# Output projection of a DiT block: operand sums formed during the attention, splits issued ahead of the sums that end a product, row steps staggered by one tile

## The chip, the cores and the metric

The kernel runs on one core of one Trainium2 chip. The metric is device time in microseconds (us) of one execution; lower is better. The core has four compute engines that the profile names PE (TensorE: matmuls; its weight loads are listed as PEld), DVE (VectorE), ACT (ScalarE) and POOL (GpSimd). SP (SyncE) issues DMAs. Each engine works through its own list of instructions strictly in order: an instruction that waits holds up all that stand behind it on the same engine. Engines meet only through semaphores, and through the buffers that one fills and another empties.

## The reference

One layer of a diffusion-transformer trunk, batch 1, 1024 latent tokens of width 1024 on a 16 x 64 grid, and 256 context tokens, all in fp32:

```python
h_x = _modulate(x, g_pre_mix[l], sh1, sc1)          # RMSNorm, then scale and shift
u_x, q_x, k_x, v_x = _project(h_x, w_in[l])         # 512 pool features; 8 heads of 64
attn_x = _neighbourhood_attention(q_x, k_x, v_x, k_c, v_c, rpb[l])
mix_x = jnp.concatenate([_pool_mixer(u_x, pool_w[l], pool_scale[l]), attn_x], axis=-1) @ w_out[l]
x = x + gt1 * _rmsnorm(mix_x, g_post_mix[l])
y_x = _sq_relu_mlp(_modulate(x, g_pre_mlp[l], sh2, sc2), w_mlp_in[l], w_mlp_out[l])
x = x + gt2 * _rmsnorm(y_x, g_post_mlp[l])
```

The change concerns the line with `w_out` (the output projection), the row step behind it (`x + gt1 * _rmsnorm(...)`), and the beginning of the MLP, whose input is that row after another RMSNorm.

## The kernel before, in words

**Arithmetic.** Every fp32 product is made of three matmuls. `split` (L143, L144) makes the high part of an operand as a cast on ScalarE and the remainder as a subtraction on VectorE; `three` (L168 to L170) multiplies high by high, high by low and low by high. A weight tile goes through `high_low`, an operand tile of the projection through `out_operand`, a token tile of the MLP through `token_part`; all three call `split`.

**The output projection.** Its input is a 2 x 2 block matrix over tokens (a: the first 512, b: the last 512) and features (512 pool features in `pools`, 512 attention features in `heads`; both lists hold four pages of 128 features by 1024 tokens). It is multiplied by the 2 x 2 blocks of `w_out` with seven block products instead of eight (Strassen-Winograd). Operand A11 is the pools' half a, A12 the heads' half a, A22 the heads' half b, and four are sums: S1 of the two halves b, S2 of S1 and A11, S4 of S2 and A12, S3 of the pools' two halves. The weights of the seven are likewise single blocks or sums. These sums are made by accumulating DMAs that GpSimd's queue issues (`add_to`): the transfer adds what it brings to what stands in the destination. A product is four output tiles of 128 tokens by 512 columns, twelve matmuls each (four feature pages, three matmuls). TensorE takes the products in this order: A11 and A12 (both into `x`), S1 (`poz`), S2 (`poy`), S4 (added to `poz`), S3 (`pov`), A22 (added to `pov`). Between them VectorE combines finished products into the quarters of the result: `u2` from `y`, `s5` from `u2` and `z`, and by `out_less` the remaining ones.

**The row step.** For a quarter of an output row tile (half h of the columns, tile t) `out_kept` takes the squares' sum on ScalarE (`mean_square`, L130) and multiplies by the gate on VectorE into the page `mp1[t]`. Once both halves are there, `row_added(t)` has the root made (`rsqrt_of`: one small operation on VectorE, then a power on GpSimd, L139), adds the gated row to the input row `xr` on VectorE (L1004), stores it by a DMA of GpSimd's queue and takes the new row's squares on ScalarE. `row_scaled(t)` makes the second root in the same way and scales the row. Then TensorE transposes the row tiles in groups of eight 128 x 128 blocks (`normal_pair`, `px`, L1080): a group of two banks is read by ScalarE with scale and shift (`nf`, L1085), and split into the token operands `th` and `tl`. `last_product` interleaves the four tiles of the product A22 with the first of these groups.

**The MLP's beginning.** The MLP uses seven products too. For the first eight blocks of 128 hidden columns, the products of the first token half come first: `first_sum` (`phx`, operand B11, token pairs 0 and 1) and `second_sum` (B21 added, token pairs 2 and 3), two blocks at a time. `first_sum` copies its bank out as `s1`. The second token half is transposed (32 transposes) and combined in `second_half`, called between these sums. The product T2 (`phy`) of block 0 opens the main part. The weights of the MLP come from SP's loads and `weight_parts`, with four split tiles made ahead (`lookahead`).

**The attention.** 32 units, four pairs of heads by eight bands of columns, one unit each 3.1 us or so; `weighed(i - 4)` writes the result of a unit to `heads[j]`, and after the last band the page of pair j ("head j") is whole. GpSimd makes the bias tables of a pair of heads ahead of it (`tables`, L660).

**What sets the order.** Inside an `in_order(...)` block the instructions of the engines named keep the order in which the code issues them. `tc.issue_after` places a block behind a given instruction. Instructions outside such blocks on an engine (the MLP's weight casts on ScalarE and VectorE, for instance) are put between them by the scheduler when the program is built, and their place is then fixed too. Around the change the blocks are: `projected` (attention and A11, A12), `added` (S1 to S3 and the first row tiles), `first_part` (A22) and `whole` (last token pair). `first` keeps TensorE's order, `first_pool` GpSimd's through the attention and the operand sums. Buffers come from rotating pools (`whl` for split weights, `page` for 1024-column pages), so a split can also wait for TensorE's last use of the buffer's earlier content.

Before the change the loop of the attention makes four copies of the pools' half b (`combined_a`, SP) and adds each pair of heads to its copy as the pair is whole, which gives S1. All further sums stand behind the attention: S2 on top of S1 in `combined_a`, S4 in the heads' half a, S3 in the pools' half a.

## Time and profile before

| | before |
|---|---|
| median of 3 runs (lowest to highest) | 1078.92 us (1078.45 to 1079.13) |
| the profiled execution | 1078.19 us, span 1076.4 us |
| mean granted TensorE clock in its span | 0.987 |
| PE busy | 1040.1 us, 97% |
| DVE / ACT / POOL busy | 713.2 us, 66% / 533.9 us, 50% / 83.9 us, 8% |
| DMA | 194.87 MB, mean 181 GB/s |

How the rows are read that follow. A row of a timeline is: start in us from the beginning of the span, duration, engine, source line, operation, output <- input by the program's names (buffer numbers left out), the shape, how many instructions were drawn together, and in brackets the engine's idle time just before, with what ended it. Matmuls overlap, so a matmul's own duration is longer than the distance to the next one; in undisturbed stretches the starts are what counts. A row of the view by windows is: the window, its length, then the busy time and the number of instructions of PE, PEld, DVE, ACT and POOL, then the granted clock of TensorE, the busy share of the DMA engines and GB/s. A row of the waits is: engine, waiting instruction, releaser, total us, times, longest. In the chain of waits a row is: start, length, step. TensorE's names in the projection: `poz` (S1, S4), `poy` (S2), `pov` (S3, A22), `px` (transposes), `phx` (first and second sums of the MLP), `phy` (T2 of the MLP). For the weights `to_0` to `to_3` and `bo_0`, h is the high part, l the low and w what was loaded.

### The profile page before, as it was taken

The numbers are of one execution on the slowest core, as the hardware profiler recorded it, in microseconds if no ns is written. First come the engines' busy times: TensorE is split into PE (matmuls) and PEld (weight loads), VectorE is DVE, ScalarE is ACT, GpSimd is POOL, SyncE is SP. The second block draws the span as 40 slices with busy tenths as digits, with TensorE's granted clock in tenths as the row PEclk, the third lists the DMA queues.
The fourth block names the chain that finished last, engine by engine and source line by source line (L and its number), as shares of the span: only waits on it lengthen the run. The fifth ranks groups of instructions, "written<-read, shape, count | busy, mean of one in ns | idle before, by whom it ended". The sixth has DMA issues, their size and how long they took to land.

```text
span 1076.4 us, 15501 instructions
## 1 busy us (share of the span) xinstructions
PE 1040.1 (97%) x5878; PEld 854.3 (79%) x5878; DVE 713.2 (66%) x1115; ACT 533.9 (50%) x927; POOL 83.9 (8%) x141
## 2 busy tenths in 40 slices
PE   8999999999999985989999999999999999999997
PEld 7788888877887764768888888888888888888885
DVE  5536646627986376689988766765577657556576
ACT  7462022257887355677555555454454334334441
POOL 2020000023201422030000000000000000000001
PEclk9999999999999988999999999999999999999999
DMA  9906753021126992673776534435597775546556
GB/s 343 316 19 212 274 178 115 29 76 42 50 70 168 203 232 83 174 237 100 267 241 205 195 122 156 163 118 188 202 381 244 256 253 183 208 158 214 176 182 209
DMA packets 104315, 194.87 MB, mean 181 GB/s; under 512 B 7984, under 2 KB 42544, under 8 KB 104240
## 3 DMA queue, kind: packets, MB, share of 16 engines
q1 hardware_dynamic: 81888, 150.82, 42.6%
q10 hardware_dynamic: 16848, 30.44, 7.7%
q0 software_dynamic: 5504, 12.61, 5.3%
q8 instruction: 46, 0.75, 0.3%
q14 instruction: 29, 0.24, 0.1%
HBM read 147.70 MB, written 38.81 MB: 173 GB/s over the span
## 4 chain that ended last, share of the span: by engine, by line
PE 88%; issue 4%; DMA 3%; ACT 2%; DVE 2%; POOL 1%; SPq 0%; POOLq 0%; DVEq 0%; ACTq 0%
PE pk L404 4%; PE S L718 3%; PE pa L794 3%; PE phx L168 3%; PE phx L170 3%; PE phx L169 3%; PE pyv L169 3%; PE pyz L170 3%; PE pyz L169 3%; PE pyx L170 3%; PE phv L168 3%; PE phz L168 3%; PE pyv L170 3%; PE pyx L168 3%; PE phz L169 3%
## 5 line engine op out<-in xcount | busy, mean ns | idle before, releaser
L1194 ACT ACTIVATE c<-c 128x512 f32<-128x512 f32 x48 | 30.3, 631 | 56.0 <-DVE c L1304 22.3
L168 PE MATMUL phx<-thB,wpA 128*128 128x512 f32 x128 | 51.1, 399 | 6.9 <-ACT s L1252 5.6
L741 ACT ACTIVATE sp<-sp,nm 128x640 f32<-128x640 f32 (+1 forms) x64 | 51.4, 803 | 8.9 <-DVE nm L732 8.6
L732 DVE CUSTOM_DVE_ANT_0 sp<-S,tab 128x640 f32<-128x640 f32 (+1 forms) x56 | 42.9, 803 | 17.3 <-PE S L718 10.4
L139 POOL TENSOR_TENSOR ry<-vy,nhalf 128x1 f32<-128x1 f32 x8 | 4.4, 550 | 594.0 <-DVE vy L137 594.0
L169 PE MATMUL phx<-tlB,wpA 128*128 128x512 f32 x128 | 50.3, 393 | 0.0
L170 PE MATMUL phx<-thB,wpA 128*128 128x512 f32 x128 | 50.3, 393 | 0.0
L144 DVE TENSOR_TENSOR wpS<-S,wpS 128x512 fp32r<-128x512 f32 x64 | 43.6, 686 | 9.3 <-ACT wpS L143 9.3
L143 ACT CAST wpS<-S 128x512 fp32r<-128x512 f32 x64 | 39.2, 616 | 19.9 <-PE phv L170 8.6
L1195 ACT ACTIVATE c<-c 128x512 f32<-128x512 f32 x48 | 30.3, 632 | 11.3 <-DVE sa L1267 10.5
L168 PEld LDWEIGHTS phx<-thB,wpA 128*128 128x128 f32 x128 | 24.4, 191 | 13.0 <-ACT s L1252 6.2
L170 PEld LDWEIGHTS phx<-thB,wpA 128*128 128x128 f32 x128 | 24.3, 190 | 5.2
L169 PEld LDWEIGHTS phx<-tlB,wpA 128*128 128x128 f32 x128 | 24.5, 191 | 4.9
L718 PE MATMUL S<-kT,q 64*128 64x384 f32 (+1 forms) x128 | 27.9, 495 | 0.4 <-DVE nm L732 0.4
L1312 DVE TENSOR_TENSOR c<-phz,u 128x512 f32<-128x512 f32 x16 | 11.0, 690 | 25.6 <-PE phz L170 25.5
L794 PE MATMUL pa<-pt,v 128*64 128x128 f32 x352 | 25.9, 279 | 0.6
L779 DVE COPY pt<-T 128x512 f32<-128x512 f32 x32 | 21.9, 686 | 5.6 <-PE T L760 5.6
L168 PE MATMUL phy<-thT,wpS 128*128 128x512 f32 x64 | 24.9, 389 | 0.0
L169 PE MATMUL phy<-tlT,wpS 128*128 128x512 f32 x64 | 24.9, 389 | 0.0
L170 PE MATMUL phy<-thT,wpS 128*128 128x512 f32 x64 | 24.9, 389 | 0.0
L168 PE MATMUL phz<-thT,wpS 128*128 128x512 f32 x64 | 24.9, 389 | 0.0
L169 PE MATMUL phz<-tlT,wpS 128*128 128x512 f32 x64 | 24.9, 389 | 0.0
(1006 smaller groups left out, 3348.0 us busy)
## 6 DMA issues: line engine op xcount, KB each, us to landing
b<-in_w SPq DMA_DIRECT2D x64, 512.0 KB, 4.5
hrS<-hdS SPq DMA_DIRECT2D x32, 512.0 KB, 5.2
hrA<-hdA SPq DMA_DIRECT2D x24, 512.0 KB, 5.8
wm<-in_w_mod SPq DMA_DIRECT2D x16, 512.0 KB, 9.6
wa_0w<-in_w SPq DMA_DIRECT2D x16, 512.0 KB, 5.0
wa_1w<-in_w SPq DMA_DIRECT2D x16, 512.0 KB, 4.1
hdA<-c ACTq DMA_DIRECT2D x32, 256.0 KB, 2.1
hdS<-sa ACTq DMA_DIRECT2D x32, 256.0 KB, 3.2
```

What stands on the lines that cost most here:

```text
L143: nc.scalar.copy(hi, src)
L144: nc.vector.tensor_tensor(lo, src, hi.bitcast(F32), sub)
L168: nc.tensor.matmul(ps, ahi, bhi, start=first, stop=False, skip_group_check=more)
L169: nc.tensor.matmul(ps, ahi, blo, start=False, stop=False, skip_group_check=more)
L170: nc.tensor.matmul(ps, alo, bhi, start=False, stop=last, skip_group_check=more)
L404: nc.tensor.matmul(pks[b][j], wk(wgt, k, low, j * P, P), r, start=(k == 0 and n == 0), stop=(k == KT - 1 and n == 2))
L718: nc.tensor.matmul(S[e][:, c0 : c0 + keys.shape[1]], q[hs, cols], keys[hs], start=True, stop=True)
L732: nc.vector.tensor_tensor_reduce(out=to, in0=s, in1=bt, scale=1.0, scalar=BIG, op0=add, op1=ALU.min, accum_out=nm)
L741: nc.scalar.activation(sp, sp, AF.Exp, bias=least[i, e], scale=-1.0, accum_out=sums[i][:, e : e + 1])
L794: nc.tensor.matmul(pa[e * HD : (e + 1) * HD, cols], v[:, f : f + HD], turns[i][:, e, c] if c < 4 else fifths[i][:, :, (e + 1) * HD : (e + ...
L1194: nc.scalar.activation(r, src, AF.Relu)
L1195: nc.scalar.activation(r, r, AF.Square)
```

## The change

Five things are done.

1. The sums are formed elsewhere and at other times. S1 is formed in place in the pools' half b (`s1a`), S3 in place in the pools' half a (`s3`, added at units 1 and 2 of the attention). `sa2` begins as a copy of S3 (SP, units 5 and 6) and takes the pair of heads, which gives S2; S4 is S2 added to the heads' half a. For pairs 0 to 2 these adds are issued in the attention's loop, at `i % 8 == 3` (S1, S2) and `i % 8 == 7` (S4); for pair 3 behind it.
2. The splits of S2 and of the last S1 operand stand among the `out_kept` steps of `x` at the end of `projected`; those of S4, S3 and A22 stand ahead of the sums that end S2, S4 and S3, so that ScalarE and VectorE come to them earlier.
3. `out_kept` is taken apart into `out_square` and `out_gated`, `row_added` and `row_scaled` give up their roots to `row_root` and `row_second`. The steps of row t - 1 are issued among those of row t. All row scalings are on VectorE (two were on ScalarE).
4. `last_rows` is gone. The steps of rows 4 to 7 move into the `added` block (half 1), into `last_product` (half 0, among the tiles of A22 and the token pairs), and into `last_pair`. The row loads 4 to 7 are issued at the end of `added`.
5. `second_half(("T2",))`, which holds the 32 transposes of the second token half, is issued ahead of the second sums of blocks 2 and 3 instead of behind them.

```diff
@@ -868,7 +868,9 @@
...
         both = [page(f"ss{i}") for i in range(2)]
-        combined_a = [both[k // 2][:, (k % 2) * 512 : (k % 2) * 512 + 512] for k in range(4)]
+        sa2 = [both[k // 2][:, (k % 2) * 512 : (k % 2) * 512 + 512] for k in range(4)]
+        s3, s1a = [p[:, :512] for p in pools], [p[:, 512:] for p in pools]
@@ -883,9 +885,6 @@
...
         first_pool.__enter__()
-        for k in range(4):
-            nc.sync.dma_start(combined_a[k], pools[k][:, 512:])
         with in_order(ET.PE, ET.Activation, ET.DVE, ET.SP) as projected:
@@ -905,7 +904,18 @@
...
                     if i % 8 == 3:
-                        add_to(combined_a[i // 8 - 1], heads[i // 8 - 1][:, 512:])
+                        j = i // 8 - 1
+                        add_to(s1a[j], heads[j][:, 512:])
+                        add_to(sa2[j], heads[j][:, 512:])
+                if i in (1, 2):
+                    for k in (2 * i - 2, 2 * i - 1):
+                        add_to(s3[k], s1a[k])
+                if i in (5, 6):
+                    for k in (2 * i - 10, 2 * i - 9):
+                        nc.sync.dma_start(sa2[k], s3[k])
+                if 8 < i < N and i % 8 == 7:
+                    j = i // 8 - 1
+                    add_to(heads[j][:, :512], sa2[j])
                 low()
@@ -942,28 +952,31 @@
...
                 if i > N:
-                    out_operand("S1", i - N - 1, combined_a[i - N - 1])
+                    out_operand("S1", i - N - 1, s1a[i - N - 1])
             low()
...
                 out_sums(x[t], "A12", [wo[2], wo[3]], t, False)
-            out_operand("S1", 3, combined_a[3])
             t2 = [out_load(f"to2_{kk}w", kk, 1, wraw) for kk in (2, 3)]
...
                 add_to(t2[i], t1[i])
+            add_to(heads[3][:, :512], sa2[3])
+            for i in range(2):
                 add_to(halved(t3[i]), out_block(i, 1))
-            for k in range(4):
-                add_to(combined_a[k], pools[k][:, :512])
             for i in range(2):
                 add_to(t4[i], t2[i])
-            for k in range(4):
-                add_to(heads[k][:, :512], combined_a[k])
-            for k in range(4):
-                add_to(pools[k][:, :512], pools[k][:, 512:])
             first_pool.__exit__(None, None, None)
             wt1 = [high_low(f"to1_{t}", t1[t]) for t in range(2)]
-            for t in range(4):
-                out_kept(0, t, x[t], att.tile([P, NKEY], F32, tag="sp", name=f"jo0_{t}", bufs=6)[:, :512])
+            junk = lambda t: att.tile([P, NKEY], F32, tag="sp", name=f"jo0_{t}", bufs=6)[:, :512]
+            out_operand("S2", 0, sa2[0])
+            out_kept(0, 0, x[0], junk(0))
+            out_operand("S2", 1, sa2[1])
+            out_operand("S1", 3, s1a[3])
+            out_kept(0, 1, x[1], junk(1))
+            out_operand("S2", 2, sa2[2])
+            out_operand("S2", 3, sa2[3])
+            for t in (2, 3):
+                out_kept(0, t, x[t], junk(t))
@@ -985,8 +998,14 @@
...
-        def out_done(h, t, c):
-            out_kept(h, t, c, out_junk(h, t))
+        def out_square(h, t, c):
+            mean_square(out_junk(h, t), c, ssm[h][:, t : t + 1])
+        def out_gated(h, t, c):
+            if t not in mp1:
+                mp1[t] = page(f"mp1_{t}")
+            hs = slice(h * 512, (h + 1) * 512)
+            nc.vector.tensor_tensor(mp1[t][:, hs], c, G1[:, hs], mul)
@@ -995,70 +1014,85 @@
...
         x1d = [dram.tile([P, D], F32, tag=f"x1_{t}", name=f"x1_{t}") for t in range(NT)]
-        rows = {}
-        def row_added(t):
-            xt = rows[t]
-            rs = rsqrt_of(f"m_{t}", ssm[0][:, t : t + 1], ssm[1][:, t : t + 1])
-            nc.vector.scalar_tensor_tensor(xt, mp1[t], rs, xt, mul, add)
-            nc.gpsimd.dma_start(x1d[t], xt)
-            ms = sm(f"sx_{t}", 1, 2)
-            mean_square(mp1[t], xt, ms)
-            return ms
+        rows, root = {}, {}
...
-        def row_scaled(t, ms):
-            rn = rsqrt_of(f"n_{t}", ms)
-            if t < 2:
-                nc.scalar.activation(mp1[t], rows[t], AF.Identity, scale=rn)
-            else:
-                nc.vector.tensor_scalar_mul(mp1[t], rows[t], rn)
+        def row_root(t):
+            root[t] = rsqrt_of(f"m_{t}", ssm[0][:, t : t + 1], ssm[1][:, t : t + 1])
+        def row_added(t):
+            xt = rows[t]
+            nc.vector.scalar_tensor_tensor(xt, mp1[t], root[t], xt, mul, add)
+            nc.gpsimd.dma_start(x1d[t], xt)
+            root[t] = sm(f"sx_{t}", 1, 4)
+            mean_square(mp1[t], xt, root[t])
+        def row_second(t):
+            root[t] = rsqrt_of(f"n_{t}", root[t])
+        def row_scaled(t):
+            nc.vector.tensor_scalar_mul(mp1[t], rows[t], root[t])
...
             z = out_bank_sums("poz", "S1", wt1)
-            for k in range(4):
-                out_operand("S2", k, combined_a[k])
-            nc.scalar.copy(s5[0], z[0])
             wt2 = out_weights("to2", t2)
-            for t in (1, 2):
-                nc.scalar.copy(s5[t], z[t])
             y = out_bank_sums("poy", "S2", wt2)
...
                 out_operand("S4", k, heads[k][:, :512])
-                if k == 0:
-                    nc.scalar.copy(s5[3], z[3])
+                if k == 1:
+                    nc.scalar.copy(s5[0], z[0])
+            for k in range(4):
+                out_operand("S3", k, s3[k])
+                if k < 3:
+                    nc.scalar.copy(s5[k + 1], z[k + 1])
             wb22 = out_weights("bo22", b22)
             for t in range(4):
+                out_operand("A22", t, heads[t][:, 512:])
                 nc.vector.tensor_tensor(u2[t], y[t], u2[t], add)
                 nc.vector.tensor_tensor(s5[t], u2[t], s5[t], sub)
-                out_operand("S3", t, pools[t][:, :512])
             wt3 = out_weights("to3", t3)
...
                 row_load(t)
-            squares = {}
+                out_sums(z[t], "S4", wb22, t, False)
+            v = out_bank_sums("pov", "S3", wt3)
+            c = {}
             for t in range(4):
-                out_sums(z[t], "S4", wb22, t, False)
-                out_done(1, t, out_less(1, t, z[t], u2[t]))
+                c[t] = out_less(1, t, z[t], u2[t])
+                out_square(1, t, c[t])
                 if t > 0:
-                    squares[t - 1] = row_added(t - 1)
-                out_operand("A22", t, heads[t][:, 512:])
+                    row_root(t - 1)
+                out_gated(1, t, c[t])
                 if t > 1:
-                    row_scaled(t - 2, squares[t - 2])
-            v = out_bank_sums("pov", "S3", wt3)
-            squares[3] = row_added(3)
-            row_scaled(2, squares[2])
-            c22 = [out_less(1, 4, s5[0], v[0])]
+                    row_second(t - 2)
+                if t > 0:
+                    row_added(t - 1)
             wt4 = out_weights("to4", t4)
-            row_scaled(3, squares[3])
-            for t in range(1, 4):
-                c22.append(out_less(1, 4 + t, s5[t], v[t]))
+            row_root(3)
+            c[4] = out_less(1, 4, s5[0], v[0])
+            row_second(2)
+            row_scaled(0)
+            row_added(3)
+            for t in (1, 2):
+                row_scaled(t)
+                c[4 + t] = out_less(1, 4 + t, s5[t], v[t])
+            row_second(3)
+            for t in (4, 5):
+                out_square(1, t, c[t])
+                out_gated(1, t, c[t])
+            row_scaled(3)
+            c[7] = out_less(1, 7, s5[3], v[3])
+            for t in (6, 7):
+                out_square(1, t, c[t])
+                out_gated(1, t, c[t])
+            for t in range(4, 8):
+                row_load(t)
@@ -1092,27 +1126,45 @@
         def last_product():
-            for t in range(4):
-                if t > 1:
-                    plain[0, t - 2] = normal_pair(0, t - 2)
-                    token_part("B11", t - 2, plain[0, t - 2])
+            def pair_made(kp):
+                plain[0, kp] = normal_pair(0, kp)
+                token_part("B11" if kp < 2 else "B21", kp % 2, plain[0, kp])
+            def first_steps(t):
+                c[t] = out_less(0, t, v[t - 4], u2[t - 4])
+                out_square(0, t, c[t])
+                out_gated(0, t, c[t])
+            def last_steps(t):
+                row_second(t)
+                row_scaled(t)
+            for t in range(2):
                 out_sums(v[t], "A22", wt4, t, False)
-            for kp in (2,):
-                plain[0, kp] = normal_pair(0, kp)
-                token_part("B21", kp % 2, plain[0, kp])
+            first_steps(4)
+            pair_made(0)
+            out_sums(v[2], "A22", wt4, 2, False)
+            row_root(4)
+            first_steps(5)
+            row_added(4)
+            pair_made(1)
+            out_sums(v[3], "A22", wt4, 3, False)
+            row_root(5)
+            first_steps(6)
+            row_added(5)
+            pair_made(2)
+            row_root(6)
+            first_steps(7)
+            row_added(6)
...
             token_part("B21", 1, plain[0, 3])
-        def last_rows():
-            for t in range(4):
-                out_done(1, 4 + t, c22[t])
-                row_load(4 + t)
-            for t in range(4):
-                out_done(0, 4 + t, out_less(0, 4 + t, v[t], u2[t]))
-                row_scaled(4 + t, row_added(4 + t))
+            row_root(7)
+            row_added(7)
+            for t in (4, 5, 6, 7):
+                row_second(t)
+                row_scaled(t)
@@ -1397,17 +1449,17 @@
...
                     with tc.issue_after(first_part[ET.DVE]), tc.issue_after(first_part[ET.Activation]):
-                        with in_order(ET.Activation, ET.DVE) as whole:
+                        with in_order(ET.Activation, ET.DVE):
                             last_pair()
-                    with tc.issue_after(whole[ET.DVE]), tc.issue_after(whole[ET.Activation]):
-                        last_rows()
-            if p > EARLY - 6:
-                second_half(("T1",) if p == EARLY - 4 else ("T3",))
+            if p == 2:
+                with in_order(ET.Activation, ET.DVE) as made_first:
+                    second_half(("T2",))
+            if p == 4:
+                second_half(("T1",))
+            if p == 6:
+                second_half(("T3",))
             for q in both:
                 second_sum(q, xs[q])
-            if p == EARLY - 6:
-                with in_order(ET.Activation, ET.DVE) as made_first:
-                    second_half(("T2",))
         second_half(("B22", "T4"))
```

## The prediction

> **What bounds the kernel now.** I read the first parts of the page, then the waits of TensorE, then the windows of the projection, then each engine's timeline there. TensorE has the span; what is left is where it stands still, and all of it that is long lies in the output projection. The waits (us in total, times, longest):
>
> ```profile
> PE 1040.1 (97%) x5878; PEld 854.3 (79%) x5878; DVE 713.2 (66%) x1115; ACT 533.9 (50%) x927; POOL 83.9 (8%) x141
> PE pov L168 <- DVE co L985: 11.8, 1, 11.8
> PE phx L168 <- ACT s L1252: 5.6, 1, 5.6
> PE poy L168 <- ACT to_0h L143: 4.2, 1, 4.2
> ```
>
> TensorE's timeline at these places, start, us, idle time before it in brackets: the first operand product, three stalls with the row at which full speed returns, and the markers I count between.
>
> ```profile
> 365.30 0.39 PE L168 MATMUL poz<-to_0h,S 128*128 128x512 f32 x1
> 380.56 0.79 PE L168 MATMUL poy<-to_0h,S 128*128 128x512 f32 x1 [4.23 <-ACT to_0h L143]
> 386.62 0.39 PE L168 MATMUL poy<-to_0h,S 128*128 128x512 f32 x1
> 394.80 0.39 PE L168 MATMUL poz<-bo_0h,S 128*128 128x512 f32 x1
> ...
> 405.68 0.39 PE L168 MATMUL pov<-to_0h,S 128*128 128x512 f32 x1
> 428.50 0.77 PE L168 MATMUL pov<-to_0h,A 128*128 128x512 f32 x1 [11.78 <-DVE co L985]
> 437.10 1.03 PE L1080 MATMUL px<-ident,mp 128*128 128x128 f32 x8
> 442.52 0.39 PE L169 MATMUL pov<-to_0l,A 128*128 128x512 f32 x1
> 446.19 0.50 PE L168 MATMUL phx<-thB,wpA 128*128 128x512 f32 x1 [0.80 <-ACT nf L1085]
> 461.86 0.79 PE L168 MATMUL phx<-thB,wpA 128*128 128x512 f32 x1 [5.57 <-ACT s L1252]
> 465.27 0.39 PE L170 MATMUL phx<-thB,wpA 128*128 128x512 f32 x1
> 477.20 3.66 PE L1080 MATMUL px<-ident,mp 128*128 128x128 f32 x32
> 480.62 0.47 PE L168 MATMUL phx<-thB,wpA 128*128 128x512 f32 x1
> 502.50 0.39 PE L168 MATMUL phy<-thT,wpS 128*128 128x512 f32 x1
> ```
>
> An undisturbed product of 48 matmuls takes 405.68 - 394.80 = 10.88, or 0.227 each. Between 365.30 and 480.62 stand five such products (S1, S2, S4, S3, A22: 54.4), eight of 12 matmuls (21.8), four groups of 8 transposes at 0.79 (3.2) and one of 32 (480.62 - 477.20 = 3.4): 82.8 of 115.3 us. So 32.5 us is the most that the change can gain here. Part of it is the clock. The twelve matmuls from 380.56 end at 386.62; less 0.47 of another wait and 2.72 of work, 2.9 are lost after a gap of 4.2 us. Eight from 461.86 end at 465.27, 1.6 lost after a gap of 5.6. The windows (PEclk is the third from the right) show the same three places:
>
> ```profile
> 376.30:394.80 18.50, 13.81 (x49) 10.84 (x49) 11.35 (x14) 11.44 (x18) 6.08 (x7) 0.82 1.10 214
> 416.70:437.10 20.40, 8.34 (x25) 6.29 (x25) 13.95 (x24) 9.67 (x15) 4.82 (x8) 0.67 0.37 120
> 449.00:477.40 28.40, 22.34 (x95) 17.73 (x94) 21.93 (x37) 20.91 (x44) 8.90 (x12) 0.94 0.86 264
> ```
>
> **The change, part by part.** The sum runs along one question: when is each operand ready, and when does TensorE come to it.
>
> *Adds moved into the attention.* The counts of POOL's DMAs are equal (16 before, 16 after), but of the thirteen that form S1 to S4 from head 3 on, three are left behind the attention: the two from head 3 at 353, and the S4 of head 3. What they cost now:
>
> ```profile
> 360.90 9.96 DMA to_3w<-to_1w
> 374.58 0.62 ACT L143 CAST S<-ss 128x512 fp32r<-128x512 f32 x1 [6.94 <-DMA ss<-y]
> 379.46 1.05 ACT L143 CAST to_0h<-to_2w 128x1024 fp32r<-128x1024 f32 x1
> 352.98 0.88 POOL L874 DMA_DIRECT2D ss<-f  x1 [21.49 <-DVE f L804]
> 360.31 0.62 ACT L143 CAST S<-ss 128x512 fp32r<-128x512 f32 x1 [4.58 <-DMA ss<-f]
> ```
>
> ScalarE stands 6.9 us for the S2 sum, and only then splits the weights for which TensorE waits at 380.56. After: S1 of head 3 lands as now (360.3); its S2 add is issued one POOL issue of 0.9 later, so by about 362; the changed program splits S1 and S2 there, before TensorE reaches 365.30 with S1 and 365.30 + 10.88 = 376.18 with S2. The S2 weights land at 360.90 + 9.96 = 370.9 at the latest (fewer transfers stand beside them); two casts and two subtractions of about 1 us each put them at 373.1, 3.1 ahead. The stall at 380.56 goes: 4.2 + 0.5 + 2.9 = 7.6.
>
> *S4, S3 and A22 split ahead of the sums.* TensorE needs S4 at 387.06, S3 at 397.94, A22 at 408.82. ScalarE and VectorE are in order: the eight S4 and S3 splits take until 378 (0.6 each on VectorE), S4's weights wait for S1's buffers (376.2) and are done at 380.5, S3's wait for S2's (387.1) and are done at 391.0. No stall. The sums of S2 (four pairs on VectorE) lie between and are off the path.
>
> *Rows a tile behind each other.* Before, row t's chain goes to GpSimd and back and VectorE waits for it, so a tile takes 5.8 us where TensorE delivers one in 2.72:
>
> ```profile
> 407.05 0.56 POOL L139 TENSOR_TENSOR rm<-vm,nhalf 128x1 f32<-128x1 f32 x1 [22.53 <-DVE vm L137]
> 412.84 0.57 POOL L139 TENSOR_TENSOR rm<-vm,nhalf 128x1 f32<-128x1 f32 x1 [3.00 <-DVE vm L137]
> 457.68 0.68 DVE L985 TENSOR_TENSOR co<-pov,so 128x512 f32<-128x512 f32 x1
> 458.88 1.28 DVE L1004 SCALAR_TENSOR_TENSOR xr<-mp,rm,xr 128x1024 f32<-128x1024 f32 x1
> ```
>
> After, the root of row t-1 is fetched during row t's gate: 1.2 for subtraction and gate (458.88 - 457.68), 1.28 for the addition and two operations on one element a row, 2.6 a tile. The steps follow TensorE: last subtraction at 398.3, third row's addition at 401, A22's weights on ScalarE 402 to 404 and on VectorE to 405.3, where TensorE wants them at 408.82. The 11.8 goes with its 0.3 and its clock loss. Next is the fourth row's scaling, which the first transposes need. The casts of the first MLP weights now stand ahead of its square on ScalarE, and they wait for buffers of S3's weights (TensorE at 407.6): square 408.5 to 409.6, root, scaling 412.7. TensorE is there at 408.82 + 5.44 = 414.26, 1.5 later. Two scalings move from ScalarE to VectorE, inside this. So the first transposes start at 414.26 instead of 437.10: **22.8 us gained**.
>
> *The second token half, step by step inside the last product.* This gives some of it back. What decides is again the built order on the in-order queues. Durations:
>
> ```profile
> 441.37 1.45 ACT L1085 ACTIVATE nf<-px,s,a 128x512 f32<-128x512 f32 x2 [1.09 <-PE px L1080]
> 442.85 1.05 ACT L143 CAST thB<-nf 128x1024 fp32r<-128x1024 f32 x1
> 443.80 0.61 ACT L143 CAST wpA<-wa2w 128x512 fp32r<-128x512 f32 x1
> 460.19 1.06 ACT L130 ACTIVATE mp<-xr 128x1024 f32<-128x1024 f32 x1 [1.01 <-DVE xr L1004]
> 443.93 1.23 DVE L144 TENSOR_TENSOR tlB<-nf,thB 128x1024 fp32r<-128x1024 f32 x1 [2.40 <-ACT thB L143]
> ```
>
> TensorE comes to the first MLP sum (phx) at 414.26 + 8.29 = 422.55 (446.19 - 0.80 - 437.10 = 8.29). On ScalarE a cast of MLP weights (wpA11_2) stands ahead of the cast of the first token pair, and it waits for the middle of A22's last tile, 420.07 (442.52 - 437.10 = 5.42 behind the first transposes, plus 0.39). From there, one behind the other: cast 0.55, token cast 1.05, its remainder on VectorE 1.14, a root's start 0.07, subtraction, weights' remainder and gate 1.8, row addition 1.3, then ScalarE's square 1.06, the second pair's two evictions 1.5, cast 1.05, remainder 1.25: 10.8 with the handovers, so the second pair is complete at 430.9. TensorE waits 1.1 for the bank of the subtraction, does six matmuls, and waits 4.65 and 1.0. Five matmuls remain: 432.0, and 1.0 more at the low clock: 433.0.
>
> The same again for the second sums: from 433.2 a weights cast (0.52, it waits for that sum to end), row 5's square 1.06, evictions 1.5, cast 1.05, remainder 1.2, subtraction, weights and gate 1.9, row 6's addition 1.3, square 1.07, evictions 1.5, cast 1.05, remainder 1.3: 13.4, the fourth pair at 446.6. TensorE has meanwhile done 8 transposes, 12 matmuls and half a sum, and stands some 1.5 and 5. Then 5 + 36 matmuls (9.3) and a clock loss: 458.2 with 2.25, the mean of 2.9 and 1.6, the two rows with gaps of like length.
>
> *The last transposes ahead of two second sums.* Rows 4 to 7 take 1.6 each through GpSimd from 446.7 on, so the last is scaled at about 455.5, 2.7 before TensorE. The 32 transposes (3.4) and two second sums (5.4) end at 467.1; before, the same work ended at 480.62. What follows needs the second half's splits; they are now ahead of the sums' evictions on ScalarE by about as much as TensorE needs, with 1 us to spare at the second sums of p = 4; if that is used up, it costs what is over. *Row loads 4 to 7* move ahead of four weight loads on SP, but behind two that wait for A22's splits (405.3): issued at 406.5 to 408.5 and, by
>
> ```profile
> DMA to landing us min/median/max: 2.9/6.5/11.8
> ```
>
> landed by 420 at the slowest, wanted at 424.7. Zero, by 4 us of cover.
>
> **Sum.** 480.62 - 467.06 = 13.5: 22.8 gained, 9.3 returned. The profiled execution took 1078.19 (span 1076.4), 0.7 under the median 1078.92 of the runs. 1078.19 - 13.5 = 1064.7; on the median, **1065.4**. Unknown is above all the clock after the two new gaps: 0 each (the row 446.19 has a gap of 0.8 and no loss) to 2.9 each, so 1061 to 1067; I take the mean of the rows whose gaps are nearest in length.
>
> [...]
>
> **Rivals.** (a) *The waits on ScalarE's queue do not bite*: if the token pairs are ready when TensorE comes, nothing of the 9.3 is returned, and up to 32.5 is gained: 1046. For it speaks that VectorE and ScalarE are busy only 13.95 and 9.67 of 20.4 us in the window at 416.70; against it that each wait above is on TensorE's own progress, fixed by buffers. Half of it, two handovers shorter than I count, gives 1060. (b) *The adds are hidden or late all the same*: the S2 weights, or the add of head 3, land after 376, and 7.6 stay; the fourth row comes late by up to 2. 1073. The row of 9.96 speaks for it, the ten transfers of 256 KB that leave this stretch against. (c) *Slower: POOL held up in the attention.* POOL now has ten more DMAs in the attention, between the tables of the heads, and an add waits there for the landing of the one before.
>
> ```profile
> 272.65 0.91 POOL L874 DMA_DIRECT2D ss<-f  x1 [4.21 <-DVE f L804]
> 289.49 5.39 POOL L660 TENSOR_TENSOR tab<-msk,U 128x128 f32<-128x128 f32 x12 [15.93 <-DMA U<-in_rpb]
> 313.45 0.69 DVE L732 CUSTOM_DVE_ANT_1 sp<-S,tab 128x512 f32<-128x512 f32 x1 [0.46 <-PE S L718]
> ```
>
> The table of head 3 is written at 289.49 to 294.9 and first read at 313.45: 18.5 us of cover. TensorE would wait from the point where POOL is 18.5 us late, and the change turns slower at 18.5 + 13.5 = 32: 1079 and more. Issues take 0.9 there and land in a few us, so little speaks for it. [...]
>
> **Chances.** Forecast (1061 to 1069) 0.55; (a) in part or whole 0.20; (b) or a like loss of up to 10 us 0.15; (c), or another loss above 13 us that I do not see, 0.10, of which 0.03 within 0.2%. The measurement tells 0.2% (2.2 us). Faster 0.90, same 0.03, slower 0.07. The range for 8 in 10 goes from 1056 to 1074.
>
> **What would show it.** Right: no wait of poy and pov over 1 us; first transposes near 414; phx with two waits of about 5 us on the token casts or their remainders (th, tl) and one of about 1 on the copy s; VectorE's row additions some 2.7 apart; the first phy at 502.50 - 13.5 = 489. Wrong: a wait of poy on DMA or its weights, of px on mp (rows late), of S on nm or tab in the attention, or no long wait of phx at all.

## The result, and the profile after

The changed kernel takes 1065.44 us (median of 4 runs, 1064.99 to 1066.35) against 1079.03 us of the kernel before beside it; the ratio is 0.9871, with a 95% interval of 0.9854 to 0.9888. The prediction said 1065.4 with a range of 1056 to 1074. The profiled execution took 1064.99 (span 1063.2), 13.2 us under the profiled one of before, where 13.5 was worked out.

The longest row of TensorE's waits from the projection on (engine, waiting instruction, releaser, us in total, times, longest):

```profile
PE phx L168 <- ACT thB L143: 9.4, 2, 5.1
```

The waits of poy and pov are gone, 16.8 us of them in the kernel before; in their place stand two waits on `thB`, the cast of a token pair. TensorE's timeline after, at the places that the prediction counts between:

```profile
365.01 0.39 PE L168 MATMUL poz<-to_0h,S 128*128 128x512 f32 x1
376.42 0.39 PE L168 MATMUL poy<-to_0h,S 128*128 128x512 f32 x1
414.50 1.03 PE L1114 MATMUL px<-ident,mp 128*128 128x128 f32 x8
423.99 0.47 PE L168 MATMUL phx<-thB,wpA 128*128 128x512 f32 x1 [1.21 <-DVE co L998]
429.89 0.80 PE L168 MATMUL phx<-thB,wpA 128*128 128x512 f32 x1 [4.27 <-ACT thB L143]
...
434.75 0.48 PE L168 MATMUL phx<-thB,wpA 128*128 128x512 f32 x1
438.95 0.50 PE L168 MATMUL phx<-thB,wpA 128*128 128x512 f32 x1 [1.19 <-ACT s L1304]
445.75 0.79 PE L168 MATMUL phx<-thB,wpA 128*128 128x512 f32 x1 [5.13 <-ACT thB L143]
...
451.73 0.40 PE L168 MATMUL phx<-thB,wpA 128*128 128x512 f32 x1
458.58 3.65 PE L1114 MATMUL px<-ident,mp 128*128 128x128 f32 x32
489.29 0.39 PE L168 MATMUL phy<-thT,wpS 128*128 128x512 f32 x1
```

S1, S2, S4, S3 and A22 follow each other without a stall, and the first transposes start at 414.50 (414.26 was forecast, 437.10 before). Then TensorE stands 4.27 us in the middle of the first phx and 5.13 in the middle of its second sum. Both times it comes back slow. From 429.89 to 434.75 it does 6 matmuls and 8 transposes, which are worth 6 x 0.227 + 0.79 = 2.15, in 4.86; less 0.47 of another wait, 2.24 are lost. From 445.75 to 451.73 it does 12 matmuls (2.72) in 5.98; less 0.47, 2.79 are lost. The last transposes start at 458.58 (458.2 forecast), the first phy at 489.29 (489).

From the first transposes to the first phy the kernel before needed 502.50 - 437.10 = 65.4 us and the changed one needs 489.29 - 414.50 = 74.8. So 22.6 us are gained ahead of the first transposes, and 9.4 returned behind them; 22.8 and 9.3 were forecast. The experiments ask which part of the change does the one and which the other. This table holds them all; "to px" is the time from the first S1 matmul to the first transposes, "px to phy" that from there to the first phy, both from each kernel's profiled execution.

| kernel | median us | ratio to before (95%) | to px | px to phy |
|---|---|---|---|---|
| before | 1078.92 | | 71.8 | 65.4 |
| changed | 1065.44 | 0.9871 (0.9854 to 0.9888) | 49.5 | 74.8 |
| adds | 1067.98 | 0.9896 (0.9881 to 0.9910) | 59.7 | 66.4 |
| no_adds | 1084.10 | 1.0044 (1.0029 to 1.0059) | 68.8 | 75.5 |
| no_adds_kept | 1084.67 | 1.0054 (1.0039 to 1.0069) | 67.4 | 75.4 |
| late_splits | 1082.48 | 1.0032 (1.0021 to 1.0043) | 65.1 | 76.0 |
| late_turn | 1065.20 | 0.9870 (0.9855 to 0.9885) | 49.3 | 74.8 |
| fill | 1064.50 | 0.9860 (0.9845 to 0.9875) | 49.6 | 73.4 |
| pairs | 1062.96 | 0.9848 (0.9834 to 0.9863) | 49.4 | 71.8 |
| four | 1058.76 | 0.9816 (0.9799 to 0.9832) | 49.0 | 67.6 |
| old_rows | 1057.83 | 0.9797 (0.9782 to 0.9811) | 49.1 | 67.0 |
| old_rows_four | 1059.30 | 0.9818 (0.9800 to 0.9837) | 49.1 | 63.8 |
| best | 1053.27 | 0.9763 (0.9747 to 0.9779) | 49.0 | 62.0 |

### The profile page after: what moved, and what is told of

The parts are those of the page before. It is cut to its first block, busy times and chain, and to the rows that moved or that the text cites. A ratio compares the mean times of both kernels' runs of the same rounds, so it can differ in the third digit from the quotient of the medians.

```text
span 1063.2 us, 15505 instructions
## 1 busy us (share of the span) xinstructions
PE 1036.0 (97%) x5878; PEld 851.4 (80%) x5878; DVE 713.7 (67%) x1117; ACT 531.4 (50%) x925; POOL 84.3 (8%) x141
## 4 chain that ended last, share of the span: by engine, by line
PE 92%; ACT 3%; DMA 2%; DVE 2%; issue 1%; SPq 0%; DVEq 0%; POOLq 0%; ACTq 0%
PE pk L404 4%; PE S L718 3%; PE pa L794 3%; PE phx L169 3%; PE pyv L168 3%; PE pyz L168 3%; PE pyx L169 3%; PE pyx L168 3%; PE phv L170 3%; PE phz L170 3%; PE phv L169 3%; PE phz L169 3%; PE pyv L170 3%; PE pyz L170 3%; PE pyv L169 3%; PE pyz L169 3%
## 5 line engine op out<-in xcount | busy, mean ns | idle before, releaser
L143 ACT CAST wpS<-S 128x512 fp32r<-128x512 f32 x64 | 39.0, 614 | 19.0 <-PE phv L170 10.2
L1247 ACT ACTIVATE c<-c 128x512 f32<-128x512 f32 x48 | 30.3, 632 | 13.2 <-DVE sa L1319 12.4
```

The source lines that it names most:

```text
L143: nc.scalar.copy(hi, src)
L1247: nc.scalar.activation(r, r, AF.Square)
```

## The experiments: what is gained ahead of the first transposes

**adds: the first part alone.** In the kernel before, the early sums and nothing else (the adds of S3, S2 and S4 in the loop as in the change):

```diff
-        combined_a = [both[k // 2][...] for k in range(4)]
+        sa2 = [both[k // 2][...] for k in range(4)]
+        s3, s1a = [p[:, :512] for p in pools], [p[:, 512:] for p in pools]
...
                     if i % 8 == 3:
-                        add_to(combined_a[i // 8 - 1], heads[i // 8 - 1][:, 512:])
+                        j = i // 8 - 1
+                        add_to(s1a[j], heads[j][:, 512:])
+                        add_to(sa2[j], heads[j][:, 512:])
...
-                out_operand("S2", k, combined_a[k])
+                out_operand("S2", k, sa2[k])
```

> The kernel before with the first part of the change alone: the sums S1 to S4 formed during the attention, everything else in its old place. By the prediction: the stall of 4.2 us at the first S2 product goes with its clock loss (7.6 us); the 11.8 us at the product A22 stay or shrink by up to 4 us, because VectorE now comes to the first row tile earlier than the product that it waits for; so 1067 to 1071.5 us. By the rival that the row chain runs from a fixed moment, the 7.6 us come back as a longer stall at A22 (19 us instead of 11.8): 1079 us. By the rival that the sums land late all the same: a wait at S2 stays, 1075 us or more.

Measured: 1067.98 us, 11.3 under the kernel before beside it (1079.28). The first transposes come 11.9 us earlier (425.18), not 7.6. TensorE's timeline, VectorE's with the first row's subtraction (402.89 in the kernel before), and VectorE's in the kernel before, where it stands for the first S2 sum:

```profile
417.53 0.77 PE L168 MATMUL pov<-to_0h,A 128*128 128x512 f32 x1 [8.40 <-DVE co L991]
425.18 1.04 PE L1086 MATMUL px<-ident,mp 128*128 128x128 f32 x8
...
391.92 0.68 DVE L991 TENSOR_TENSOR co<-poz,so 128x512 f32<-128x512 f32 x1
...
375.23 0.69 DVE L144 TENSOR_TENSOR S<-ss,S 128x512 fp32r<-128x512 f32 x1 [6.87 <-ACT S L143]
```

The stall at S2 is gone, and TensorE comes to S3 7.6 us earlier (398.09, 405.68 before), as the prediction counted. But the stall at A22 is 8.40 instead of 11.78, because the row chain has gained more than TensorE: VectorE too had stood behind the late sums (6.87 us for the first S2 sum alone). It splits the weights of S2 8.2 us earlier (372.37, 380.54 before) and those of S4, behind the late S4 sums, 11.0 (379.65, 390.62); the first row and A22 come 11.0 earlier too. The last 0.9 is a shorter slow stretch behind the stall at A22 (7.65 us from its end to the transposes instead of 8.60). So one part of five already gives 11.3 of the 13.6 us, and the four others together add 2.5 us to it. The next three kernels look at the others from the other side.

**no_adds: everything but the first part.** The copies of the pools, the adds in the loop and those behind the attention are the old ones:

```diff
-        s3, s1a = [p[:, :512] for p in pools], [p[:, 512:] for p in pools]
+        s3, s1a, sa2 = [p[:, :512] for p in pools], combined_a, combined_a
...
+            out_operand("S1", 3, combined_a[3])
             t2 = [out_load(f"to2_{kk}w", kk, 1, wraw) for kk in (2, 3)]
```

> The changed kernel with its first part undone: the sums S2, S3 and S4 are formed behind the attention again, the splits and row steps stay as changed. Theory: the S2 sums land at 374 to 378 as before, the splits that now stand ahead in the queues wait for them, and with them the steps that free the banks of the S1 product; TensorE stands some 5 us in S1, again at S2, with a clock loss: 1072 to 1077 us. If the parts only add up, the 11.3 us that the sums alone gave are lost: 1076.7 us. Rival, that the staggered rows make up for it: under 1070 us.

Measured: 1084.10 us, slower than the kernel before. TensorE's wait in S1 was twice what I expected:

```profile
PE poz L168 <- DVE mp L860: 10.8, 1, 10.8
```

ScalarE's timeline has the reason:

```profile
374.59 0.62 ACT L143 CAST S<-ss 128x512 fp32r<-128x512 f32 x1 [11.54 <-DMA ss<-y]
```

It waits 11.54 us for the first S2 sum, with the steps that free the banks of `x` queued behind it.

**no_adds_kept: the S2 splits taken back behind those steps.**

```diff
-            out_operand("S2", 0, sa2[0])
-            out_kept(0, 0, x[0], junk(0))
-            out_operand("S2", 1, sa2[1])
-            out_kept(0, 1, x[1], junk(1))
...
+            for t in range(4):
+                out_kept(0, t, x[t], junk(t))
+            for t in range(4):
+                out_operand("S2", t, sa2[t])
```

> The kernel without the early sums (S2, S3 and S4 formed behind the attention), with one order taken back as well: the four splits of S2 stand behind the steps of x again, no longer among them. Theory: the 10.8 us that TensorE stood in the S1 product came from these splits, which waited for sums that had not landed and held up the steps that free its banks. Then that wait is gone, the stall of before at S2 (4 to 5 us with its clock loss) takes its place, the rows' stagger keeps its gain at A22: first transposes near 423, 1071 to 1076 us, faster than before without the early sums. Rival, that the staggered rows need the early sums whatever the order: waits of the same sum elsewhere, 1081 us or more.

Measured: 1084.67 us. My theory fell. The wait of 10.8 is gone, but the first transposes come only 1.4 us earlier (67.4 instead of 68.8), since other waits took its place: 3.84 at S2, 2.97 at S4, 3.52 at A22. ScalarE's timeline shows why:

```profile
396.08 0.62 ACT L143 CAST S<-y 128x512 fp32r<-128x512 f32 x1 [0.52 <-DMA y<-y]
396.60 1.04 ACT L143 CAST bo_0h<-bo_2w 128x1024 fp32r<-128x1024 f32 x1
410.66 0.63 ACT L130 ACTIVATE jo<-co 128x512 f32<-128x512 f32 x1 [8.09 <-DVE co L989]
```

The last S3 sum lands at 396.1, and in the changed order the weights of S4 (`bo_0h`) and everything of the rows stand behind its split.

**late_splits: the S3 splits taken back too**, each behind the sum of its tile as in the kernel before; the staggered rows and what follows stay.

```diff
-            for k in range(4):
-                out_operand("S3", k, s3[k])
-                if k < 3:
-                    nc.scalar.copy(s5[k + 1], z[k + 1])
+            for k in range(3):
+                nc.scalar.copy(s5[k + 1], z[k + 1])
...
                 nc.vector.tensor_tensor(s5[t], u2[t], s5[t], sub)
+                out_operand("S3", t, s3[t])
```

> The kernel just tried without the early sums, with the splits of S3 taken back too: each stands behind the sum of its tile, and the weights of S4 no longer wait behind them on ScalarE. What is left of the change's first half is the stagger of the rows. Theory: without early sums the S3 sums land at 390 to 396; split ahead, they hold up the weights of S4 (3.0 us at 397.7) and all that follows on VectorE, the rows too (first row at 410.7 where the kernel before had 402.9). Taken back, the first row starts near 404, the wait at S4 goes and the stagger gains: first transposes near 423, 1072 to 1077 us. Rival, that the stagger gains nothing by itself because the row chains of before waited for other things: first transposes at 432 or later, 1081 us or more.

Measured: 1082.48 us, the rival's time. The wait at S4 is gone and the first transposes come earlier, as the theory had it, but at 430.61, not near 423 and a little ahead of the rival's 432, and the whole is slower than the kernel before. VectorE's timeline has the first row's subtraction, in the kernel before

```profile
402.89 0.68 DVE L985 TENSOR_TENSOR co<-poz,so 128x512 f32<-128x512 f32 x1
```

and here, with the additions behind it:

```profile
407.18 0.68 DVE L989 TENSOR_TENSOR co<-poz,so 128x512 f32<-128x512 f32 x1
410.38 1.28 DVE L1020 SCALAR_TENSOR_TENSOR xr<-mp,rm,xr 128x1024 f32<-128x1024 f32 x1 [0.46 <-POOL rm L139]
413.45 1.29 DVE L1020 SCALAR_TENSOR_TENSOR xr<-mp,rm,xr 128x1024 f32<-128x1024 f32 x1 [0.40 <-POOL rm L139]
```

The stagger works: additions are 3.1 us apart, where a row took 5.8 before. But it starts 4.3 us later: four splits of A22 (0.6 each) now stand ahead of it on VectorE, and the weights of S4 are split 1.9 us later. So without the early sums the stagger is worth 6.7 us on the way to the first transposes (71.8 to 65.1). With them it is worth 10.2 (59.7 to 49.5, the splits' order included). It then loses 10.6 behind the transposes (76.0 instead of 65.4). That time from px to phy is much the same in all kernels with the changed order of rows 4 to 7, early sums or not: 74.8 to 76.0.

## The experiments: what is returned behind them

**pairs: the second token pair ahead of row 4.** In `last_product`, with `first_steps` taken apart into `taken` (the subtraction, which frees a bank) and `kept_steps` (square and gate):

```diff
-            first_steps(4)
-            pair_made(0)
-            out_sums(v[2], "A22", wt4, 2, False)
-            row_root(4)
-            first_steps(5)
-            row_added(4)
-            pair_made(1)
+            taken(4)
+            kept_steps(4)
+            taken(5)
+            pair_made(0)
+            out_sums(v[2], "A22", wt4, 2, False)
+            pair_made(1)
...
+            row_root(4)
+            kept_steps(5)
+            row_added(4)
```

> The changed kernel with one order changed: inside the last product the second token pair (eviction, cast, remainder) stands ahead of the addition of row 4, the two subtractions that free banks stand earlier, and row 5 and 6 follow behind. Theory: the long waits of phx come from the order that is written on ScalarE and VectorE, token pairs behind the rows' chains. Then the wait of 4.3 us at the first phx falls under 2 us and its clock loss goes, phx0 is complete near 428 instead of 433.4, the second long wait stays at 5 to 7 us; 1060 to 1063 us. Rival 1, the casts of MLP weights ahead of the token casts hold them up: they stay where they are, the wait stays over 3 us, 1064 us or more. Rival 2, ScalarE and VectorE have too much work altogether here: what the first wait loses the second gains, 1065 us.

Measured: 1062.96 us. Three of the four casts of MLP weights that stood ahead of the second token cast on ScalarE still stand there, the first of them behind TensorE at 420.44 as before (420.35); the first long wait is 0.63 on the cast (and 0.76 on its remainder) instead of 4.27, and no clock is lost there (0.39 or 0.40 a matmul from 426.98 on). In its place stands a smaller one at the third pair (1.54, and 0.76 on its remainder), and the last has grown from 5.13 to 6.32. TensorE's timeline:

```profile
425.38 0.50 PE L168 MATMUL phx<-thB,wpA 128*128 128x512 f32 x1 [0.63 <-ACT thB L143]
426.64 0.50 PE L169 MATMUL phx<-tlB,wpA 128*128 128x512 f32 x1 [0.76 <-DVE tlB L144]
442.89 0.79 PE L168 MATMUL phx<-thB,wpA 128*128 128x512 f32 x1 [6.32 <-ACT thB L143]
```

**old_rows: rows 4 to 7 behind the token pairs.** Part 4 undone, the stagger kept: `last_rows` is called behind `last_pair` as in the kernel before, loads the rows itself, and takes roots, additions and scalings of rows t - 1 and t - 2 among the steps of row t:

```diff
-            for t in (4, 5):
-                out_square(1, t, c[t])
-                out_gated(1, t, c[t])
...
+        def last_rows():
+            for t in range(4, 8):
+                out_square(1, t, c[t])
+                out_gated(1, t, c[t])
+                row_load(t)
+            for t in range(4, 8):
+                c[t] = out_less(0, t, v[t - 4], u2[t - 4])
+                out_square(0, t, c[t])
...
```

> The changed kernel with its fourth part undone: the steps of rows 4 to 7 (both halves, and their loads) stand behind the last token pair again, a tile behind each other as in the changed kernel; the rest as changed. Theory: the rows' chains ahead of the token pairs make the two long waits. Undone, the token pairs are ready when TensorE comes (no long wait on th), and the one long wait of before on the copy s (5.6 us) is back; from the first transposes to the first phy it takes the 66 us of the kernel before instead of 74.8: phy near 481, 1056 to 1060 us. Rival 1, that the rows' work is the bound wherever it stands: the wait on s, or one at the 32 transposes, grows by the 9 us that are saved: 1064 us or more. Rival 2, that MLP weight casts hold up the token casts: the waits on th stay.

Measured: 1057.83 us, 7.6 under the changed kernel; from px to phy 67.0 us, 7.8 less. TensorE's timeline, the one long wait with the end of its slow stretch, and the first phy (481 expected):

```profile
440.53 0.80 PE L168 MATMUL phx<-thB,wpA 128*128 128x512 f32 x1 [7.13 <-ACT s L1298]
...
444.09 0.39 PE L170 MATMUL phx<-thB,wpA 128*128 128x512 f32 x1
...
481.20 0.39 PE L168 MATMUL phy<-thT,wpS 128*128 128x512 f32 x1
```

No wait on a token cast is left, only the long one on the copy `s` and two short ones (0.80 and 0.48) on evictions. So the two new waits of the changed kernel come from the rows' steps that stand ahead of the token pairs on ScalarE and VectorE. Rival 1 (the same work is the bound wherever it stands) is right for a small part: the wait on `s` is 7.13 us instead of 5.57, since the copy now stands behind the rows. Rival 2 (the casts of MLP weights) this run alone does not exclude, because in the built order these casts moved behind the first token casts too. For the first wait `pairs` excludes it as the main cause; for the second the changed kernel's ScalarE does, which has no weight cast from 438.4 to the token cast at 444.65, but stands 1.67 us for a row addition.

**four: other work for TensorE in the second wait.** Weights, first sums and second sums go in groups of four, two and two blocks, and the 32 transposes stand behind the second sums of blocks 0 to 3:

```diff
-            for p in range(0, EARLY, 2):
-                both = [weight_parts(q, ("A11", "A12")) for q in (p, p + 1) if q < EARLY]
+            for g in ((0, 1, 2, 3), (4, 5), (6, 7)):
+                both = [weight_parts(q, ("A11", "A12")) for q in g]
...
```

> The changed kernel with TensorE's order changed: the first sums of blocks 2 and 3 stand ahead of the second sums of blocks 0 and 1 (and the 32 transposes behind the second sums of blocks 0 to 3), so that 24 matmuls that need nothing new fill the second long wait. Theory: the wait of 5.1 us falls to about 2, no clock is lost there, the transposes start at about 457 with two sums less left behind them: phy at about 482, 1057 to 1060 us. Rival, that the fourth token pair is late because ScalarE follows TensorE: the copies of the two added sums stand on ScalarE ahead of its cast, the wait stays at 5 us or moves on to the transposes (rows 4 to 7 late): 1063 us or more.

Measured: 1058.76 us, 6.7 under the changed kernel. The fourth token pair is no earlier (its cast ends the wait at 446.24, against 445.75), but TensorE has done 24 matmuls more by then and waits 0.44, and 0.77 on the remainder (the first long wait stays, 4.28); the last transposes have two sums less behind them, and the first phy comes at 482.23 (482 expected):

```profile
446.24 0.49 PE L168 MATMUL phx<-thB,wpA 128*128 128x512 f32 x1 [0.44 <-ACT thB L143]
482.23 0.39 PE L168 MATMUL phy<-thT,wpS 128*128 128x512 f32 x1
```

**late_turn: the fifth part undone.**

```diff
-            if p == 2:
-                with in_order(ET.Activation, ET.DVE) as made_first:
-                    second_half(("T2",))
...
             for q in both:
                 second_sum(q, xs[q])
+            if p == 2:
+                with in_order(ET.Activation, ET.DVE) as made_first:
+                    second_half(("T2",))
```

> The changed kernel with one part undone: the 32 transposes of the second token half stand behind the second sums of blocks 2 and 3 again. By the prediction this part moves TensorE's work and no wait, since the last row is scaled about 3 us before TensorE comes: the transposes start 5.4 us later with two sums less behind them, and the first phy is where it was: 1064.5 to 1066.5 us. The rival, that the splits of the second half need the two sums as cover: some waits of th and tl at phy or at the sums of blocks 4 to 7, 1068 us or more.

Measured: 1065.20 us, the changed kernel's time. The transposes start at 464.51, and the first phy 74.8 us behind the first transposes as in the changed kernel. This part moves work and no wait.

**fill: is it the standstill that makes TensorE slow?** The repeated matmuls give the same sums.

```diff
-            for k in range(4):
+            more = name == "B11" and not filled
+            filled.append(1)
+            for k, end in ((0, 0), (1, 1)) * (3 if more else 0) + ((0, 0), (1, 0), (2, 0), (3, 1)):
...
-                      begin and k == 0, k == 3, more=not begin)
+                      begin and k == 0, bool(end), more=not begin)
```

> The changed kernel with the first six matmuls of the first phx done three times more, on the same operands with the same result, so that TensorE works through most of its first long wait (18 matmuls of 0.227 us: 4.1 of 4.3 us). Theory: the 2.2 us that the next matmuls and transposes lose (0.43 us each instead of 0.23) come from the standstill; without it they run at 0.23, phx0 is complete about 1.2 us earlier, at 432.2, and the whole about 1.2 us faster: 1064.2 us. Rival, the matmuls after the wait are slow for another reason (weights or operands that arrive late): 0.43 each all the same, 1065.4 us or more.

Measured: 1064.50 us, 0.9 under the changed kernel, with intervals that overlap; TensorE's timeline decides:

```profile
429.99 0.51 PE L168 MATMUL phx<-thB,wpA 128*128 128x512 f32 x1 [0.18 <-ACT thB L143]
431.25 0.50 PE L169 MATMUL phx<-tlB,wpA 128*128 128x512 f32 x1 [0.75 <-DVE tlB L144]
433.31 0.48 PE L168 MATMUL phx<-thB,wpA 128*128 128x512 f32 x1
```

The token pair comes at the same moment (429.99, 429.89), the matmuls behind it run at full speed (0.39 or 0.40 each from 431.59 on), and the next phx starts at 433.31 instead of 434.75. Less their waits for the remainder (0.75, and 0.47 in the changed kernel), the same six matmuls and eight transposes take 2.57 us instead of 4.39. So 1.8 of the 2.24 us were the price of standing still; the other 0.4 is lost at full speed too. At the first phy 1.3 us are left of the gain (487.96).

**old_rows_four and best: the two orders together.** The first joins `old_rows` and `four`.

> The kernel just described with the first sums of blocks 2 and 3 ahead of the second sums of blocks 0 and 1. Theory: the 24 matmuls cover the wait on the copy s too, so 2 to 3 us are left of it; first phy near 475, 1050 to 1055 us, the fastest so far. Rival, that rows 4 to 7 are then late for the 32 transposes: a wait of px on mp of 4 us or more, 1056 us or more.

Measured: 1059.30 us, no better than either. The first phy starts early, at 477.65, but now TensorE's longest waits are there:

```profile
PE phy L168 <- ACT wpS L143: 2.8, 1, 2.8
PE phy L170 <- DVE wpS L144: 2.3, 1, 2.3
```

The first weights of the main part (`wpS`) stand on ScalarE behind three of four token casts that TensorE needs much later, the next ones behind all four. `best` puts these behind:

```diff
-        second_half(("B22", "T4"))
         parts = lookahead([sequence()], 4)
+        rest = [("B22",), ("T4",)]
...
-            block_pair(0, lambda: None)
+            block_pair(0, lambda: rest and second_half(rest.pop(0)))
```

> The kernel with rows 4 to 7 behind the token pairs and the first sums of blocks 2 and 3 ahead, with the splits of the operands B22 and T4 issued inside the first block of the main part instead of ahead of it. Theory: the two waits at the first phy (2.8 and 2.3 us, and the slow matmuls behind them) come from these four casts of 1 us, which stood on ScalarE ahead of the first weights of the main part. Then the first phy starts near 475 without a wait over 1 us: 1051 to 1054 us, below all others. Rival, that ScalarE and VectorE have no room left there and the wait moves on to B22 or T4 (phz, phv): 1057 us or more.

Measured: 1053.27 us (1052.97 to 1053.40), ratio 0.9763 (0.9747 to 0.9779): it beats both kernels, by 25.6 us the one before beside it (1078.82) and by 12.2 the changed one. TensorE's first phy, and one wait behind it:

```profile
475.97 0.39 PE L168 MATMUL phy<-thT,wpS 128*128 128x512 f32 x1
488.65 0.50 PE L169 MATMUL phv<-tlT,wpA 128*128 128x512 f32 x1 [1.41 <-DVE tlT L144]
```

The longest wait that is left behind the first transposes is 2.19 us, and one of 1.41 on T4's splits shows that these are now just late.

## Why the prediction was right, and where it was not

*The stall at S2* went, as said. The weights were split when the prediction set it, though the transfer took 10.80 us where 9.96 stood; it was issued 1.8 earlier. The chain of waits holds it:

```profile
359.12 10.80 DMA to_3w<-to_1w
```

The cast and the remainder behind it, from the timelines of ScalarE and VectorE:

```profile
369.95 1.05 ACT L143 CAST to_1h<-to_3w 128x1024 fp32r<-128x1024 f32 x1 [1.58 <-DMA to_3w<-to_1w]
371.76 1.22 DVE L144 TENSOR_TENSOR to_1l<-to_3w,to_1h 128x1024 fp32r<-128x1024 f32 x1
```

Split by 373.0, wanted at 376.42: 3.4 us ahead, 3.1 forecast.

*The price of the early sums* is the step that failed. "The stall at 380.56 goes: 4.2 + 0.5 + 2.9 = 7.6" counted TensorE's standstill, and rightly (adds: 7.6 at S3), but not that VectorE stood for the same sums. Alone, the early sums bring 11.9 us to the first transposes. In the total it did not show: 22.8 us were worked out from TensorE's own work with no stall left, and 22.6 measured. That total was sound; its division into 7.6 for the sums and 15.2 for the rest was not. A prediction of one of the two parts alone would have been wrong by 4 us or more, and for the stagger alone it would have had the wrong sign: 15.2 - 9.3 is a gain of 5.9 us, and late_splits is 3.5 us slower than the kernel before beside it (1078.96).

*The stagger's pace* was set too short, and with it one sign of being right was missed: 2.6 us a tile ("some 2.7 apart"), where the row additions start 3.08 apart in the changed kernel. VectorE still stands some 0.4 us a tile for the root from GpSimd, which the sum had at nothing. The first two additions, on VectorE:

```profile
395.09 1.29 DVE L1029 SCALAR_TENSOR_TENSOR xr<-mp,rm,xr 128x1024 f32<-128x1024 f32 x1 [0.46 <-POOL rm L139]
398.17 1.28 DVE L1029 SCALAR_TENSOR_TENSOR xr<-mp,rm,xr 128x1024 f32<-128x1024 f32 x1 [0.40 <-POOL rm L139]
```

It cost nothing, because A22's weights had cover: split by 407.0 (405.3 forecast), wanted at 409.06.

*The fourth row's scaling* was not 1.5 us ahead of TensorE: forecast to be done at 412.7, it ran from 413.87 to 414.62 (behind a root that took 1.53 us on GpSimd), and the transposes began at 414.50. No wait shows there, but the margin was gone. VectorE's and GpSimd's timelines:

```profile
413.87 0.75 DVE L1038 TENSOR_SCALAR mp<-xr,rn 128x1024 f32<-128x1024 f32 x1 [0.46 <-POOL rn L139]
412.31 1.53 POOL L139 TENSOR_TENSOR rn<-vn,nhalf 128x1 f32<-128x1 f32 x1 [1.81 <-DVE vn L135]
```

*The second half inside the last product* went step by step as forecast. ScalarE around the first long wait, without the evictions at 427.33:

```profile
420.35 0.62 ACT L143 CAST wpA<-wa2w 128x512 fp32r<-128x512 f32 x1 [1.17 <-PE pov L169]
426.27 1.06 ACT L130 ACTIVATE mp<-xr 128x1024 f32<-128x1024 f32 x1 [1.67 <-DVE xr L1029]
...
428.79 1.04 ACT L143 CAST thB<-nf 128x1024 fp32r<-128x1024 f32 x1
```

The cast of weights that waits for A22 (420.35), the square of row 4, the evictions, the cast at 428.79: the pair complete at 431.1, 430.9 forecast. The waits of 1.1, 4.65 and 1.0 at the first place measured 1.21, 4.27 and 0.47, those of 1.5 and some 5 at the second 1.19, 5.13 and 0.47. The clock losses have to be counted as the sum counts them, from the moment a pair is complete (the 2.24 and 2.79 above begin at the first matmul behind the wait, so they hold part of what the sum calls a wait). From 431.15 five matmuls and eight transposes take 3.60 us for 1.92 of work: 1.7 lost, where 1.0 stood, since the transposes run slowly too (eight from 433.45 to 434.75, 1.30 us instead of 0.79). From 447.00 to 458.58 41 matmuls take 11.58 for 9.31: 2.3, where 2.25 stood.

*Which link of that chain is the cause* the prediction left open and named the weight cast first. The runs say: it is the row chain (old_rows takes 7.8 us from px to phy, pairs 3.0), while the weight cast's own share is at most the 1.17 us of its wait and 0.5 of its length.

*The clock.* The prediction took the loss behind the two new gaps from the rows of the nearest gaps in the kernel before; neither of those gaps was broken as the second one is here (1.2, six matmuls, 5.1). The clock fell there too: the granted clock is 0.50 from 444.8 to 451.5, and most of the twelve matmuls behind the gap start 0.43 us apart. The nearest gaps were a good guide, 0.7 us too low in all. The 1061 to 1067 is worked out on the profiled execution; on the median it is 0.7 higher.

*Rival (a)*, that the waits do not bite, was wrong for this order. Another order comes near its half way (1060): in old_rows the token pairs are ready when TensorE comes, and it takes 1057.83. *Rival (b)* did not occur. *Rival (c)* neither: the tables of head 3 are written when they were before (289.57, 289.49), and an add issued right behind another one takes 1.17 us, by GpSimd's timeline:

```profile
273.25 1.17 POOL L876 DMA_DIRECT2D ss<-f  x1
289.57 5.39 POOL L660 TENSOR_TENSOR tab<-msk,U 128x128 f32<-128x128 f32 x12 [9.49 <-DMA U<-in_rpb]
```

## What to carry to other kernels

Count a stall for every engine that stands in it: an operand that comes late holds up the queue behind it on ScalarE and VectorE as well (6.87 us of VectorE for the first S2 sum in the kernel before), and the next stall shrinks with it (at A22 11.78 us before, 8.40 in adds). An order that issues work ahead is only as good as its inputs: with the sums late, the same splits "ahead" cost 3.7 us on the way to the first transposes (no_adds against late_splits). Work of a later stage that is moved into an earlier one belongs behind what the matmul engine waits for next; here the same row steps cost 7.6 us more ahead of the token pairs than behind them.

## What the hardware showed that was not expected

TensorE did not always come back slow from a standstill in these runs; it also turned slow later, amid work, or not at all. First best, after a wait of 2.19 us, then old_rows_four after the same wait (TensorE's timelines; matmuls at full speed have 0.39 or 0.40 in the second column, at the half clock 0.63):

```profile
432.60 0.50 PE L168 MATMUL phx<-thB,wpA 128*128 128x512 f32 x1 [2.19 <-DVE co L998]
432.93 0.39 PE L169 MATMUL phx<-tlB,wpA 128*128 128x512 f32 x1
433.16 0.55 PE L170 MATMUL phx<-thB,wpA 128*128 128x512 f32 x1
433.51 0.63 PE L168 MATMUL phx<-thB,wpA 128*128 128x512 f32 x1
...
436.49 0.48 PE L169 MATMUL phx<-tlB,wpA 128*128 128x512 f32 x1
436.81 0.40 PE L170 MATMUL phx<-thB,wpA 128*128 128x512 f32 x1
...
432.51 0.50 PE L168 MATMUL phx<-thB,wpA 128*128 128x512 f32 x1 [2.19 <-DVE co L998]
...
433.33 0.40 PE L168 MATMUL phx<-thB,wpA 128*128 128x512 f32 x1
```

In best the matmuls from 433.51 to 436.49 start 0.42 or 0.43 us apart, those from 436.81 on 0.22 to 0.24, so the slow stretch begins and ends while the matmuls stand back to back; the mean granted clock from 413.90 to 450.60 is 0.95 there. In old_rows_four the starts stay 0.22 to 0.24 apart from 432.86 to 440.62. In pairs two waits with one matmul between them (1.54 and 0.76 us) have the same effect as in best: from 435.09 to 435.94 the matmuls take 0.63. Nor does the loss grow with the wait in these runs: 4.27 us in the changed kernel cost 2.24, 5.13 cost 2.79, and 7.13 in old_rows 1.7 (eight matmuls from 440.53 to 444.09, 3.56 us for 1.82 of work).

The granted clock in slices of 0.1 us shows what was lost. In the changed kernel it is at 0.50 from 427.65 to 434.48 and from 444.72 to 451.54. Both stretches begin inside a wait, where the one in best begins behind it. Of the first, 4.59 us are left when work resumes at 429.89, of the second 5.79 from 445.75; less the wait of 0.47 in each, half of the rest is 2.1 and 2.7, by estimate nearly all of the 2.24 and 2.79 lost. In these two the loss follows what is left of the slow stretch when work resumes, not the length of the wait alone. What sets the moment at which a stretch begins or ends the runs do not show.
